# Leaving the k/v blocks of the second chunk out of the convolution's pacing account

## The chip, the cores and the metric

The kernel runs on one core of a Trainium2 chip. The metric is device microseconds of one execution, less is better. Engines are named as in the profile: PE (TensorE matmul), PEld (its weight loads), DVE (VectorE), ACT (ScalarE), POOL (GpSimd), SP (SyncE, whose queue issues the DMAs here).

## What is computed

One layer of a hybrid encoder over 16 meta tokens, a prompt of 256 tokens and a sample of 2048 tokens, all in float32. Cut to what matters:

```
h = rmsnorm(z)
q, k, v, g_att, c_val, c_glu, g_conv = split(h @ w_in)      # 1024 -> 2816 columns
att = windowed_gqa(rmsnorm(q), rmsnorm(k), v, sink) * silu(g_att)
u   = c_val * sigmoid(c_glu)
cnv = silu(layernorm(depthwise_conv31(u) + conv_b)) * silu(g_conv)
out = z + concat(att, cnv) @ w_out
```

The attention has 8 query heads and 2 key/value heads; a token sees the 16 meta tokens and the tokens at most 128 away. The convolution is 31 taps wide and runs per channel over 512 channels; its LayerNorm runs over the channels of a token.

## The kernel before

**Tiling.** The tokens stand in 18 blocks of 128 (b = 0 to 17), in six groups of three blocks, in two chunks of three groups. The input projection has eleven units of 256 columns; each matmul has float32r operands that are split in a high and a low part, three passes for each of eight slices of the 1024 inputs, so one output tile is 24 matmuls. For each chunk the program goes through the units in this order: four convolution units, two convolution gates, two attention gates, the k/v unit, two q units. `kv_group` calls `kv_block` for each block of 128 tokens: 24 matmuls into the PSUM tile pj, the norm of k (squares on ACT, `rsqrt` on POOL), the split and store of v, and in the next two ticks kn on DVE, a transpose kt on PE, ks on ACT and DVE, and the store to kd. In the second chunk it is called for blocks 9 to 17.

**Convolution.** For each chunk and each of four channel tiles, `conv` puts 31 taps in a queue; a tap is one DVE instruction over 128x1167 (line 946). They aren't written at once: `tick(ns)` is called after each piece of PE work with the time that the piece is taken to last, and pays taps from that credit; `owe(ns)` charges the credit with other DVE work, here 800 for a k/v block:

```
    def tick(ns):
        credit[0] += LOAD * ns
        if ln_q and not flushing[0] and ln_q[0][0]():
            ln_q.pop(0)[1]()
            ...
            credit[0] -= 800
        while credit[0] > 0 and (conv_q[0] or conv_q[1]):
            ...
            credit[0] -= cost
            f()
        credit[0] = min(credit[0], 0.0)
```

`tick` also writes what `later(k, f)` has put off by k ticks.

**LayerNorm of the convolution.** When the last taps of a chunk are written, `ready()` becomes true a set number of ticks later (one, for the second chunk), and each further tick writes one block of `ln_block`: four transposes lnt on PE (line 221), statistics on DVE, `rsqrt` on POOL, then in the next tick zn on DVE (line 234), then four transposes lnu back (line 240), SiLU on ACT into the same tile zn, and then the store of zn to the DRAM tile cd on SP (line 246). zn has three buffers, so the zn of a block waits for the store of the block three before it. There are ten such blocks in the second chunk.

**What stands around it.** After the fourth block of the last q unit but one, `attention_open` frees the convolution's space and loads the attention's constants, among them bias (1520 KB, line 269), then q, kw and v tiles. The first attention blocks are woven into the last q units: scores S (line 383), the exponential on ACT, a scaling on POOL (line 479), transposes pT_c, pT_m, pT_x (lines 495 and 499), their split in high and low by ACT and DVE (lines 515 and 516), the products O with v (line 533). When the projections are done, `attention_rest` goes on with attention and output projection y (line 609). For the boundary blocks pT_x is split and then spread by POOL (line 507); pm, which pT_x reads, has one buffer (line 470). cn on POOL (line 579) is the gate of the convolution half, mch and mcl its split (lines 586 and 587).

**What sets the order.** The instructions of an engine run in program order. That order is made by a scheduler at build time that moves instructions past each other after a time model of its own; POOL from `attention_open` on, and PE from `attention_rest` on, keep the order in which the program is written. All DMAs are issued by SP, in order, in eight lanes: an issue waits until the eighth before it has landed.

Of the kernel before, what the change touches and what calls it, by code (L numbers as in the profile page):

```python
# [85 lines left out]
CHUNKS = [[0, 1, 2], [3, 4, 5]]  # L86
# [13 lines left out]
def hymba_kernel(  # L100
# [58 lines left out]
    def owe(ns):  # L159
        credit[0] -= ns  # L160

    def later(k, f):
        due.setdefault(clock[0] + k, []).append(f)
# [30 lines left out]
    def store(dst, src):  # L194
        later(2, lambda: nc.sync.dma_start(dst, src))
# [505 lines left out]
    if True:  # L701
# [171 lines left out]
        def proj_te(ws, g, o, rows):  # L873
            x = xg[g]
            ps = pj()
            k = 0
            for d in range(ND):
                for wi, xi in PASSES:
                    nc.tensor.matmul(  # L879
                        ps[:rows, :UW],  # L880
                        x[xi][:, d, o : o + rows],
                        ws[:, d, wi, :],
                        start=(k == 0),
                        stop=(k == 3 * ND - 1),
                    )
                    k += 1
            return ps
# [87 lines left out]
        def head_norm(ps, rows, nh, tag, late=False):  # L975
            ss = gp.tile([P, 4], F32, tag="ss", name=f"ss{tag}", bufs=4)
            if phase[0] == 2 or tag.startswith("q0_9") or tag.startswith("q0_1"):
                sq = gp.tile([P, 4, HD], F32, tag="sq4", name=f"sq{tag}", bufs=2)
                sqf = sq.rearrange("p h e -> p (h e)")[:rows, : HD * nh]
                nc.scalar.activation(sqf, ps[:rows, : HD * nh], AF.Square)  # L980
                nc.vector.tensor_reduce(ss[:rows, :nh], sq[:rows, :nh, :], axis=AX.X, op=ALU.add)
            else:
                sq = gp.tile([P, 4, HD], F32, tag="sq4", name=f"sq{tag}", bufs=2)[:, 0, :]
                for h in range(nh):
                    nc.scalar.activation(  # L985
                        sq[:rows], ps[:rows, HD * h : HD * h + HD], AF.Square, accum_out=ss[:rows, h : h + 1]
                    )
            rq = gp.tile([P, 4], F32, tag="rq", name=f"rq{tag}", bufs=4)
            if late:
                later(late, lambda: rsqrt(rq[:rows, :nh], ss[:rows, :nh], 1.0 / HD, EPS))  # L990
            else:
                rsqrt(rq[:rows, :nh], ss[:rows, :nh], 1.0 / HD, EPS)
            return rq
# [29 lines left out]
        def kv_block(ws, g, o, rows, b):  # L1023
            ps = proj_te(ws, g, o, rows)
            rk = head_norm(ps, rows, KV, f"k{b}")
            vs = sp.tile([P, KV, 2, HD], F32R, tag="vs", name=f"vs{b}", bufs=3)
            pv = ps[:rows, P : 2 * P].rearrange("p (h e) -> p h e", e=HD)
            nc.scalar.copy(vs[:rows, :, 0, :], pv)
            nc.vector.tensor_tensor(vs[:rows, :, 1, :], pv, vs[:rows, :, 0, :], op=ALU.subtract)
            vflat = vs[:rows].rearrange("p a b e -> p (a b e)").bitcast(F32)  # L1030
            store(vmd if b < 0 else vd[b], vflat)
            kn = sp.tile([P, KV, HD], F32, tag="kn", name=f"kn{b}")
            owe(800)

            def fin():
                pk = ps[:rows, 0:P].rearrange("p (h e) -> p h e", e=HD)
                nc.vector.tensor_tensor(  # L1037
                    kn[:rows],
                    pk,
                    rk[:rows, :KV].unsqueeze(2).to_broadcast([rows, KV, HD]),  # L1040
                    op=ALU.mult,
                )
                later(1, fin2)

            def fin2():
                pt = psum.tile([P, 512], F32, tag="d", name=f"kt{b}")
                nc.tensor.transpose(pt[:, :rows], kn[:rows].rearrange("p a e -> p (a e)"), ident[:rows, :rows])
                ks = sp.tile([P, 2 * P], F32R, tag="ks", name=f"ks{b}")
                nc.scalar.mul(ks[:, :rows], pt[:, :rows], kscale[:, 0:1])
                nc.vector.scalar_tensor_tensor(  # L1050
                    ks[:, rows : 2 * rows], pt[:, :rows], kscale[:, 0:1], ks[:, :rows], op0=ALU.mult, op1=ALU.subtract
                )
                to = (kmd if b < 0 else kd[b]).rearrange("(h p) k l n -> p h k (l n)", h=2)
                for kv in range(KV):
                    part = ks[HD * kv : HD * kv + HD, : 2 * rows].bitcast(F32)
                    store(to[:, :, kv, :], part.unsqueeze(1).to_broadcast([HD, 2, 2 * rows]))

            later(1, fin)

        def kv_group(ws, g):  # L1060
            if g == 0:
                kv_block(ws, 0, 0, NM, -1)
                tick(24 * 107)
            for b in range(3 * g, 3 * g + 3):
                kv_block(ws, g, blk_local(b)[1], P, b)
                tick(24 * 110)
# [248 lines left out]
```

## Time and profile before

| what | value |
|---|---|
| median of 3 runs | 943.96 us (943.12 to 943.99) |
| profiled execution | 943.95 us, of which the span of the trace is 941.9 us |
| PE busy | 935.6 us, 99% of the span |
| DVE busy | 744.4 us, 79% |
| ACT busy | 421.8 us, 45% |
| POOL busy | 293.3 us, 31% |
| granted TensorE clock | 1.000 |

The span runs from the first to the last instruction; the 2.05 us between it and the execution's time lie around it. Busy time of PE is the time in which at least one matmul is in flight; matmuls overlap each other, so that a short hold of PE hardly shows in it and is read from the starts of matmuls that follow each other.

### The profile page before, as it was taken

To read this page: it belongs to the slowest core of one execution; us is meant where nothing else is said; L and a number is where in the kernel's file an instruction comes from. 1 tells how busy PE (TensorE), PEld (TensorE's weight loads), DVE (VectorE), ACT (ScalarE), POOL (GpSimd) and SP (SyncE) were. 2 spreads that over 40 slices of the span, in tenths; PEclk is the share of its full clock that TensorE was granted. 3 is DMA by queue.
4 is the path that set the end of the run, shared out by engine and by line. 5 is a ranking of instruction groups with operands and counts; after the bars stand their busy time and mean duration, and the time that the engine had idled before them with its cause. 6 is when DMAs were issued, how large, how long until landed. Compare 5 with 4: busy or idle time off the path is not lost.

```text
span 941.9 us, 16665 instructions
## 1 busy us (share of the span) xinstructions
PE 935.6 (99%) x5794; PEld 886.3 (94%) x5794; DVE 744.4 (79%) x1263; ACT 421.8 (45%) x1160; POOL 293.3 (31%) x490
## 2 busy tenths in 40 slices
PE   9999999999999999999999999999999999999998
PEld 8999999999999999999999999988888888888887
DVE  5579999997977879999996655677777677767773
ACT  7432022253457751011111356666666666656661
POOL 4320000173558400000000553755433242333332
PEclk9999999999999999999999999999999999999999
DMA  8575345676656595233333697975666556655512
GB/s 306 170 253 217 134 176 176 217 269 251 182 185 189 182 312 182 90 113 134 140 128 123 159 327 225 395 240 159 200 188 172 151 165 196 188 159 148 163 62 68
DMA packets 146211, 176.49 MB, mean 187 GB/s; under 512 B 40816, under 2 KB 108736, under 8 KB 146000
## 3 DMA queue, kind: packets, MB, share of 16 engines
q1 hardware_dynamic: 146128, 175.43, 57.8%
q8 instruction: 46, 0.75, 0.3%
q14 instruction: 37, 0.30, 0.1%
HBM read 112.69 MB, written 62.70 MB: 186 GB/s over the span
## 4 chain that ended last, share of the span: by engine, by line
PE 94%; DMA 2%; DVE 1%; SPq 1%; issue 0%; ACT 0%; POOL 0%; DVEq 0%; ACTq 0%; POOLq 0%
PE pj L863 43%; PE y L609 21%; PE pj L879 13%; PE O L533 5%; PE S L383 4%; PE pT_c L499 2%; PE pT_m L499 2%; PE pT_x L499 1%; DMA cd<-zn 1%; DMA bias<-in_bias_c 1%; PE qT L383 1%; PE lnu L240 0%; DMA xn<-in_z 0%; PE lnt L221 0%; DVE xt L772 0%
## 5 line engine op out<-in xcount | busy, mean ns | idle before, releaser
L863 PE MATMUL pj<-xh,ws 128*128 128x384 f32 (+1 forms) x1536 | 395.9, 338 | 0.1
L946 DVE SCALAR_TENSOR_TENSOR y<-us,cw,y 128x1167 f32<-128x1167 f32 x240 | 329.0, 1427 | 0.4
L863 PEld LDWEIGHTS pj<-xh,ws 128*128 128x128 f32 x1536 | 280.0, 188 | 0.4 <-ACT xh L1111 0.4
L863 PE MATMUL pj<-xl,ws 128*128 128x384 f32 (+1 forms) x768 | 260.9, 340 | 0.1
L609 PE MATMUL y<-wo,rest 128*128 128x512 f32 (+1 forms) x672 | 172.7, 394 | 0.0
L879 PE MATMUL pj<-ws,xh 128*128 128x256 f32 (+1 forms) x880 | 164.2, 284 | 0.3 <-DVE kn L1037 0.3
L863 PEld LDWEIGHTS pj<-xl,ws 128*128 128x128 f32 x768 | 144.1, 188 | 0.5 <-DVE xl L801 0.4
L609 PEld LDWEIGHTS y<-wo,rest 128*128 128x128 f32 x672 | 117.5, 189 | 21.4 <-DVE rest L566 0.3
L879 PEld LDWEIGHTS pj<-ws,xh 128*128 128x128 f32 (+1 forms) x880 | 136.1, 187 | 1.1 <-issue 0.4
L879 PE MATMUL pj<-ws,xl 128*128 128x256 f32 (+1 forms) x440 | 124.3, 283 | 0.0
L441 DVE CUSTOM_DVE_ANT_0 sb<-S,bias,vec 128x304 f32<-128x304 f32 (+5 forms) x144 | 74.5, 517 | 33.8 <-PE S L383 31.5
L453 ACT ACTIVATE sb<-sb,nm 128x304 f32<-128x304 f32 (+5 forms) x144 | 77.8, 540 | 48.9 <-DVE nm L441 48.2
L971 ACT ACTIVATE go<-pj 128x384 f32<-128x384 f32 x48 | 23.5, 489 | 149.8 <-PE pj L863 142.3
L879 PEld LDWEIGHTS pj<-ws,xl 128*128 128x128 f32 (+1 forms) x440 | 82.2, 187 | 0.2
L479 POOL TENSOR_SCALAR sb<-sb,es 128x304 f32<-128x304 f32 (+5 forms) x144 | 73.1, 525 | 16.0 <-DVE es L466 13.1
L561 POOL TENSOR_TENSOR at<-at,ga 128x256 f32<-128x256 f32 x36 | 26.5, 737 | 164.0 <-DVE at L555 104.8
L148 POOL TENSOR_SCALAR ssk<-ssk 128x2 f32<-128x2 f32 x18 | 8.4, 465 | 210.0 <-ACT sqk L985 210.0
L383 PEld LDWEIGHTS S<-kw,q 128*128 128x128 f32 x288 | 53.2, 188 | 10.6
L383 PE MATMUL S<-kw,q 128*128 128x304 f32 (+5 forms) x288 | 62.8, 299 | 0.0
L148 POOL TENSOR_SCALAR ssq<-ssq 128x4 f32<-128x4 f32 (+2 forms) x55 | 23.5, 427 | 98.3 <-ACT xn L726 74.4
L906 ACT ACTIVATE sg<-pj 128x384 f32<-128x384 f32 (+1 forms) x24 | 11.8, 492 | 82.9 <-PE pj L863 82.0
L609 PE MATMUL y<-wo,mch 128*128 128x512 f32 x144 | 47.2, 409 | 0.0
(139 smaller groups left out, 1306.9 us busy)
## 6 DMA issues: line engine op xcount, KB each, us to landing
wd<-ws SPq DMA_DIRECT2D x36, 512.0 KB, 5.8
ws<-wd SPq DMA_DIRECT2D x36, 512.0 KB, 6.2
wraw<-in_w_in SPq DMA_DIRECT2D x52, 256.0 KB, 6.3
xn<-in_z SPq DMA_DIRECT2D x18, 512.0 KB, 5.5
gd<-go SPq DMA_DIRECT2D x48, 192.0 KB, 2.2
yo<-in_z SPq DMA_DIRECT2D x36, 256.0 KB, 3.9
out_y<-yo SPq DMA_DIRECT2D x35, 256.0 KB, 2.7
wo<-wod SPq DMA_DIRECT2D x16, 512.0 KB, 7.4
```

Of the source, the lines that this page charges most:

```text
L148: nc.gpsimd.tensor_scalar(src, src, scale, eps, op0=ALU.mult, op1=ALU.add)
L383: r = f(*a, **k)
L441: nc.vector.tensor_tensor_reduce(out=sb[:, n, c0:c1], in0=ps[:, 0:w], in1=cst["bias"][:, kv, at + c0 : at + c1], scale=1.0, scalar=nsnk[:, ...
L453: nc.scalar.activation(sb[:, n, c0:c1], sb[:, n, c0:c1], AF.Exp, bias=nm[:, n : n + 1], scale=-1.0, accum_out=rs[:, n : n + 1],)
L479: nc.gpsimd.tensor_scalar(sb[:, k, a0:a1], sb[:, k, a0:a1], es[:, k : k + 1], 1.0, op0=ALU.mult, op1=ALU.mult)
L499: nc.tensor.transpose(pt[: c1 - c0, n, :], sbt[b, kv][:, n, c0:c1], ident)
L533: nc.tensor.matmul(opj[b, kv][:, n0:n1], t[:r, kv, :], p[:r, n0:n1], start=(k == "c" and i == 0), stop=(k == "x" and i == len(work) - 1),)
L561: nc.gpsimd.tensor_tensor(at[:, pr, :], at[:, pr, :], gat[b][:, pr, :], op=ALU.mult)
L609: nc.tensor.matmul(ps, mh[mi][:, e % 4, :], wo[e, wi][:, cols], start=(e == 4 and k == 0), stop=(e == 3 and k == 2),)
L863: nc.tensor.matmul(ps[:, :n], ws[:, d, wi, P * half_i : P * half_i + P], x[xi][:, d, o : o + n], start=(k == 0), stop=(k == 3 * ND - 1),)
L879: nc.tensor.matmul(ps[:rows, :UW], x[xi][:, d, o : o + rows], ws[:, d, wi, :], start=(k == 0), stop=(k == 3 * ND - 1),)
L946: nc.vector.scalar_tensor_tensor(y[:, yo + o0 : yo + o1], u[:, o0 + k : o1 + k], cw[:, j, k : k + 1], y[:, yo + o0 : yo + o1], op0=ALU.mul ...
```

## The change

`kv_block` charges its 800 to the credit only for the blocks of the first chunk.

```
             kn = sp.tile([P, KV, HD], F32, tag="kn", name=f"kn{b}")
-            owe(800)
+            owe(800 if g in CHUNKS[0] else 0)
```

The same instructions are issued, as many on each engine; their order differs on all five. Three places follow, each before and then after.

PE, at the end of the fifth k/v block of the second chunk (pj is the projection's tile, lnt the first LayerNorm transposes), before:

```order
L879 MATMUL pj_5333<-ws_8_4916,xl_3263 128x256
L879 MATMUL pj_5333<-ws_8_4916,xh_3262 128x256
L879 MATMUL pj_5378<-ws_8_4916,xh_3484 128x256
L879 MATMUL pj_5378<-ws_8_4916,xl_3485 128x256
L879 MATMUL pj_5378<-ws_8_4916,xh_3484 128x256 x2
```

and after:

```order
L879 MATMUL pj_5333<-ws_8_4916,xl_3263 128x256
L879 MATMUL pj_5333<-ws_8_4916,xh_3262 128x256
L221 MATMUL lnt_5369<-ident,y_0_3778 128x128
L221 MATMUL lnt_5369<-ident,y_1_3984 128x128
L221 MATMUL lnt_5369<-ident,y_2_4332 128x128
L221 MATMUL lnt_5369<-ident,y_3_4720 128x128
L879 MATMUL pj_5392<-ws_8_4916,xh_3484 128x256
```

The first LayerNorm block stands one k/v block, 24 matmuls, earlier. The order of the taps themselves on DVE, and the instructions that stand between the last of them, are the same before and after.

SP, around the load of bias (cd takes the finished LayerNorm blocks; the first of its stores here is the fifth of ten), before:

```order
L269 DMA bias<-in_bias_c 128x6080
L317 DMA vc_5856<-vd 128x256
L317 DMA vm_5857<-vd 128x256
L329 DMA q_6092<-qd 128x512
L195 DMA qd<-qs_11_5762 128x256
L300 DMA kw_5836<-kd 128x4x128 x2
L317 DMA vc_6570<-vd 128x256
L317 DMA vm_6571<-vd 128x256
L195 DMA qd<-qs_12_5821 128x256
L246 DMA cd<-zn_5703 128x512
```

and after:

```order
L269 DMA bias<-in_bias_c 128x6080
L317 DMA vc_5880<-vd 128x256
L317 DMA vm_5881<-vd 128x256
L246 DMA cd<-zn_5667 128x512
L195 DMA qd<-qs_11_5786 128x256
L329 DMA q_6093<-qd 128x512
L300 DMA kw_5860<-kd 128x4x128 x2
L246 DMA cd<-zn_5727 128x512
```

The fifth store to cd moves from the tenth to the third issue behind bias, the sixth from the fourteenth to the eighth.

PE, at the end of the input projection (S, pT and O belong to the first two attention blocks, y to the output projection), before; the 24 matmuls of the last projection tile, pj_6583, stand ahead of the first row, and the transposes pT_c_6621 and pT_m_6643 ahead of those:

```order
L879 MATMUL pj_6583<-ws_7_5574,xh_3484 128x256
L383 MATMUL S_1_1_6648<-kw_5836,q_1_6311 128x240 x2
L533 MATMUL O_1_6651<-ptiles,vc_5856 128x512
L533 MATMUL O_0_6467<-ptiles,vm 128x512
L533 MATMUL O_1_6651<-ptiles,vc_5856 128x512
L533 MATMUL O_1_6651<-ptiles,vm_5857 128x512
```

and after:

```order
L879 MATMUL pj_6583<-ws_7_5598,xh_3484 128x256
L499 MATMUL pT_c_6621<-ident,sb_5872 128x128 x4
L383 MATMUL S_1_0_6629<-kw_5860,q_1_6311 128x272 x2
L499 MATMUL pT_m_6643<-ident,sb_5872 128x128 x4
L383 MATMUL S_1_1_6648<-kw_5860,q_1_6311 128x240 x2
L533 MATMUL O_0_6467<-ptiles,vm 128x512
L533 MATMUL O_1_6651<-ptiles,vc_5880 128x512 x2
L533 MATMUL O_1_6651<-ptiles,vm_5881 128x512
```

The transposes have moved behind the last projection tile, right ahead of the products O_1 that read their split.

DVE at the same place, before:

```order
L441 ISA sb_5844,nm_1_6626<-S_1_0_6629,bias,vec 128x272
L441 ISA nm_1_6626 128x1
L465 TENSOR_TENSOR es_0_6414<-es_0_6414,rs_0_6413 128x4
L466 RECIPROCAL es_0_6414<-es_0_6414 128x4
L981 TENSOR_REDUCE ssq_16_6560<-sqq_16_6561 128x4
L516 TENSOR_TENSOR ptiles<-pT_c_6621,ptiles 128x512
L516 TENSOR_TENSOR ptiles<-pT_m_6643,ptiles 128x512
L587 TENSOR_TENSOR mcl<-cn_6257,mch 128x512
```

and after:

```order
L465 TENSOR_TENSOR es_0_6414<-es_0_6414,rs_0_6413 128x4
L466 RECIPROCAL es_0_6414<-es_0_6414 128x4
L981 TENSOR_REDUCE ssq_16_6560<-sqq_16_6561 128x4
L587 TENSOR_TENSOR mcl<-cn_6257,mch 128x512
L441 ISA sb_5868,nm_1_6626<-S_1_0_6629,bias,vec 128x272
L441 ISA nm_1_6626 128x1
L516 TENSOR_TENSOR ptiles<-pT_c_6621,ptiles 128x512
```

mcl and the scores' step of S_1_0 now stand ahead of the split of pT_c. On ACT, likewise, mch has moved from behind the two casts of line 515 to ahead of them; POOL's order at this place is the same.

## Rows read from the trace of the kernel before

**Rows 1.** The page: the span, and busy time of each engine.
```profile
span 941.9 us, 16665 instructions
...
PE 935.6 (99%) x5794; PEld 886.3 (94%) x5794; DVE 744.4 (79%) x1263; ACT 421.8 (45%) x1160; POOL 293.3 (31%) x490
```

**Rows 2.** Stretch: length, busy of PE, PEld, DVE, ACT, POOL; clock; DMA share, GB/s.
```profile
560.00:580.00 20.00, 19.30 (x164) 18.91 (x164) 9.24 (x20) 11.28 (x32) 8.23 (x20) 1.00 0.73 231
```

**Rows 3.** Timeline of PE (start, length): ahead of the eighth and tenth lnu.
```profile
567.31 0.28 PE L879 MATMUL pj<-ws,xh 128*128 128x256 f32 x1
567.64 0.66 PE L240 MATMUL lnu<-ident,zn 128*128 128x128 f32 x4
...
574.29 0.28 PE L879 MATMUL pj<-ws,xh 128*128 128x256 f32 x1
575.22 0.63 PE L240 MATMUL lnu<-ident,zn 128*128 128x128 f32 x4 [0.66 <-DVE zn L234]
```

**Rows 4.** Timeline of DVE: the eighth and tenth zn, and what they waited for.
```profile
566.77 0.81 DVE L234 TENSOR_SCALAR zn<-lnt,mv 128x512 f32<-128x512 f32 x1 [3.07 <-DMA cd<-zn]
...
574.27 0.81 DVE L234 TENSOR_SCALAR zn<-lnt,mv 128x512 f32<-128x512 f32 x1 [4.00 <-DMA cd<-zn]
```

**Rows 5.** Timeline of SP: issues behind bias; the last is the fifth store to cd.
```profile
552.29 0.70 SPq L269 DMA_DIRECT2D bias<-in_bias_c  x1
...
553.99 0.43 SPq L329 DMA_DIRECT2D q<-qd  x1
...
561.77 0.33 SPq L317 DMA_DIRECT2D vm<-vd  x1
...
562.93 0.36 SPq L246 DMA_DIRECT2D cd<-zn  x1
```

**Rows 6.** DMA views around 552.3 and 554.0: KB, us from issue to landing.
```profile
bias<-in_bias_c SPq DMA_DIRECT2D x1, 1520.0 KB, 9.5
...
q<-qd SPq DMA_DIRECT2D x1, 256.0 KB, 9.1
```

**Rows 7.** Chain that ended last, pieces (start, length): PE's pace.
```profile
531.36 0.44 PE lnt L221 x4
...
602.26 2.84 PE pj L879 x24
```

**Rows 8.** Timeline of PE: the ninth lnt.
```profile
562.15 0.60 PE L221 MATMUL lnt<-ident,y 128*128 128x128 f32 x4
```

**Rows 9.** Timeline of DVE: the last tap of the convolution.
```profile
522.75 1.42 DVE L946 SCALAR_TENSOR_TENSOR y<-us,cw,y 128x1167 f32<-128x1167 f32 x1
```

**Rows 10.** Timeline of POOL: from the release of pm to line 507.
```profile
597.56 0.40 POOL L470 TENSOR_TENSOR pm<-sb,es 128x128 f32<-128x128 f32 x1 [1.77 <-issue]
...
601.21 1.28 POOL L579 TENSOR_TENSOR cn<-cn,gc 128x512 f32<-128x512 f32 x1
602.45 1.22 POOL L507 TENSOR_TENSOR ptiles<-ptiles,vec 128x512 fp32r<-128x512 f32 x1
```

**Rows 11.** Timeline of ACT: the cast mch.
```profile
604.86 0.63 ACT L586 CAST mch<-cn 128x512 fp32r<-128x512 f32 x1
```

**Rows 12.** Timeline of DVE: the scores' step of S_1_0, split of pT_c, mcl.
```profile
602.70 0.49 DVE L441 CUSTOM_DVE_ANT_0 sb<-S,bias,vec 128x272 f32<-128x272 f32 x1
...
604.13 0.68 DVE L516 TENSOR_TENSOR ptiles<-pT_c,ptiles 128x512 fp32r<-128x512 f32 x1
...
605.53 0.69 DVE L587 TENSOR_TENSOR mcl<-cn,mch 128x512 fp32r<-128x512 f32 x1
```

**Rows 13.** Timeline of PE: pT_x of the first block, then around the last projection tile.
```profile
597.15 0.27 PE L495 MATMUL pT_x<-ident,pm 128*128 128x128 f32 x1
...
604.94 0.39 PE L383 MATMUL S<-kw,q 128*128 128x240 f32 x2
605.16 0.40 PE L533 MATMUL O<-ptiles,vc 128*128 128x512 f32 x1
605.39 0.39 PE L533 MATMUL O<-ptiles,vm 128*128 128x512 f32 x1
605.62 0.40 PE L533 MATMUL O<-ptiles,vc 128*128 128x512 f32 x1
```

## The prediction

> **What bounds the kernel now.** I read the page first: PE is busy 99% of the span and DVE 79% [rows 1]. So the end is set by the stream of matmuls, and the change, which adds and takes away no instruction, can only move the time by the holds of PE between matmuls. Next I looked for those in the stretch that the change reorders, from about 510 us to 610 us, by stages: one stage of 20 us, from 560 us, is the only one in which PE isn't busy throughout, 19.30 of 20.00 [rows 2]. The timeline of PE there shows two holds, both ahead of a LayerNorm transposition lnu. A matmul of the projection starts 2.84 / 24 = 0.118 us after the one before it [rows 7]; ahead of the eighth lnu 567.64 - 567.31 = 0.33 us pass, 0.21 too many, and ahead of the tenth 575.22 - 574.29 = 0.93, 0.81 too many [rows 3]. Together 1.02 us: all that this stretch can give back. Who held them: zn on DVE, which itself waited for a store to cd, 3.07 us and 4.00 us, to free its buffer [rows 4]. And that store was late because SP stood still: the eighth issue behind bias is issued at 561.77, when bias lands (552.29 + 9.5 = 561.8), and the fifth store to cd comes two issues after that, at 562.93 [rows 5, 6].
>
> **The change, part by part.** *The taps.* The diff means to let the last taps follow each other on DVE. The order says that the scheduler had already put them as it puts them now: the last tap ran at 522.75 for 1.42 us [rows 9], with the same neighbours before and after. Worth nothing. What does change is that `ready` comes a tick sooner, so all ten LayerNorm blocks stand one k/v block earlier against PE's stream. The first lnt moves from 531.36 to 531.36 - 24 x 0.118 = 528.5; the last tap ends at 524.2, so 4.3 us of cover are left [rows 7, 9]; were that cover gone, PE would wait for the tap itself.
>
> *The eighth lnu.* In the order before, 41 matmuls stand between the ninth lnt and the eighth lnu, now 11, with as many transpositions ahead as before. PE arrives at 562.15 + 0.44 + 11 x 0.118 = 563.9 [rows 7, 8], some 3.5 us sooner than it did. Its zn must be done by then, and for that the fifth store must have landed. On SP this store is now the third issue behind bias. The third issue before was q, of the same 256 KB, and it landed at 553.99 + 9.1 = 563.1 [rows 5, 6]. I take that for the store. Then zn runs from 563.2 to 564.0 (0.81 us, [rows 4]), lnu goes at 564.06 (before, 567.64 - 567.58 = 0.06 after zn, [rows 3, 4]), and PE waits about 0.2 us. Bounds: 0, if bias lands half a microsecond sooner; 1.0, if it lands 0.8 us later, since the weights ahead of it are asked for when PE ends the k/v unit, and two more groups of transpositions (0.44 us each, [rows 7]) now stand ahead of that point.
>
> *Does the queue keep its order?* The landings of bias and q follow their issue [rows 5, 6]. The Trainium skill, in "DMA: Bandwidth & Descriptors", section "Queues, rings and completion order", says that completion is not in order for one issuing engine; by that rule the store could land ahead of bias, and the sum would lose its 0.2 us.
>
> *The ninth and tenth lnu.* Bias to q is 512 KB (two transfers of 128 KB and q) in 1.3 us, 394 KB per us [rows 5, 6]. The sixth store is the eighth issue behind bias, so issued at 561.8; behind the fifth store lie 896 KB and its own 256 KB, 2.9 us: it lands at 566.0, its zn ends near 566.9. PE arrives 23 matmuls and two groups later, 564.06 + 2.7 + 0.88 = 567.6 [rows 7]. The seventh store stands 768 KB further: 566.0 + 2.6 = 568.6, its zn ends at 569.5, PE arrives at 567.6 + 0.44 + 31 x 0.118 = 571.7. No wait at either, 0.7 and 2.2 us to spare, by estimate. So of the 1.02 us about 0.8 come back.
>
> *The end of the projection.* Here the change costs. Before, the transpositions pT_c and pT_m of the second attention block's half stood ahead of the last projection tile, whose 24 matmuls, 2.84 us [rows 7], hid their split on ACT and DVE. Now they stand behind it, and between pT_c and the products O_1 lie only two S, pT_m and one O. Measured from pT_x of the first half (597.15, [rows 13]): PE needs 0.11 for it, 0.23 for an O, 41 x 0.118 = 4.85 for the projection, 0.22 for an S (605.16 - 604.94), and pT_c starts at 5.4; then 0.44, 0.22, 0.44, 0.22 bring O_0 at 6.7, and two O of 0.23 (605.62 - 605.39) bring the second O_1, which reads the low part, at 7.2 [rows 7, 13]. POOL is released by the same pT_x and runs through: line 579 ends 602.49 - 597.15 = 5.3 after it, line 507 at 603.67, 6.5 after it [rows 10, 13]. O_0 needs line 507: 0.2 to spare. The low part needs, on ACT and DVE in the new order, mch (0.63, to 5.95), mcl (0.69, to 6.65), the scores' step of S_1_0 (0.49, to 7.15) and the split of pT_c (0.68, to 7.8) [rows 11, 12]. So PE waits about 0.6 us. Before, that split ended at 604.81 and its O came at 605.62 [rows 12, 13]. Bounds: 0, if DVE's four steps overlap or POOL starts sooner; 1.3, if POOL's chain comes 0.7 later, for then O_0 waits too. It can't be below nothing, as nothing here held PE before. Behind this place the attention's order is the same again, save one O and a few loads; I count nothing for it.
>
> *Sum*, against the profiled execution of 943.95 us, which is the median of the runs to 0.01: 943.95 - 1.02 + 0.2 + 0.6 = 943.7.
>
> **The rivals.**
> *Both waits gone.* The fifth store lands in time and the split of pT_c isn't late: 943.95 - 1.02 = 942.9. For it: both of my waits are a few tenths on a chain of five or six rows. Against it: DVE's four steps in a row are in the order, and POOL's release hangs on pT_x.
> *Nothing happens to the time.* What the LayerNorm gives, the end of the projection takes to the tenth, or the early blocks are held by bias as much as before: 943.95. It can't be told from the forecast by the time, only by the rows.
> *Slower: the eighth lnu is early and its store is not.* If the fifth store lands as late as before, just ahead of 566.77 [rows 4], PE, which now comes 3.5 us sooner, stands from 563.9 to 567.64: 3.7 us, and the time is 943.95 - 1.02 + 3.7 + 0.6 = 947.2. This counts as slower (above 945.84) once lnu waits over 2.3 us, that is, once the store lands after 565.3. For it: the store waits for SiLU of the fifth block, and all of SP's queue waits behind it. Against it: it needs 2.2 us more than the row of q gives.
> *More waits at both ends*, short of that: 1.0 and 1.3 in place of 0.2 and 0.6 give 945.2.
>
> **How the numbers follow.** The forecast, with waits within some tenths of mine, 0.69; both gone 0.12; waits near their upper bounds 0.08; the slower rival 0.08; something that I don't see and that gains over 0.2%, 0.03, as no hold of that size is in the stretch. The range reaches from the case with both waits gone to just short of their upper bounds, 942.9 to 945.0. A measurement of this kernel can tell about 0.2%, 1.89 us, from no change: faster 0.03, within 0.2% 0.89, slower 0.08.
>
> **What would show it.** In the changed profile: the taps as before; the first lnt near 528.5; no hold of PE ahead of the tenth lnu, and a few tenths at the eighth; the fifth store issued within a few us of bias and landing about 1.3 us behind it; pT_c right behind the last projection matmul, and the second O_1 some 0.6 us late, with the split of pT_c on DVE ending just ahead of it. I am wrong if PE holds over 1 us ahead of any lnu, if the O_1 products run without a gap, or if a wait turns up in the k/v blocks, where LayerNorm's statistics now stand among one more block's kn and v.

## The result, and the profile after

The changed kernel took 945.7 us (median of 16 runs, 943.98 to 947.47), the kernel before 943.96 (16 runs beside them, 943.09 to 944.86): a ratio of 1.0019, interval 1.0012 to 1.0027. It is slower, by about 1.7 us, where 943.7 was forecast with a range up to 945.0. Two later comparisons of the same two kernels gave 1.0014 (1.0002 to 1.0026) and 1.0017 (1.0007 to 1.0027), with medians 0.55 and 1.56 us apart. (Every ratio is the one on record, with its 95% interval; it is not the quotient of the two medians.)

The page of the profiled execution, which took 946.34 us (span, busy time):

```profile
span 944.4 us, 16656 instructions
...
PE 937.2 (99%) x5794; PEld 888.2 (94%) x5794; DVE 744.9 (79%) x1263; ACT 422.1 (45%) x1160; POOL 295.5 (31%) x490
```

Busy shares say as little as before [rows 1]. Two things move the span. The first projection matmul starts at 13.15 us here and at 12.20 in the profile before: 0.95 us of the 2.5 between the spans lie in the head of the program, which the change doesn't touch (in the later profiles it starts between 12.17 and 13.26 whichever kernel it is). Counted from there, the span is 931.3 us after and 929.7 before: 1.6 us, close to the difference of the medians. These lie in two holds, that is, delays of PE read from the starts of matmuls that follow each other. The view of what PE waited for (us in total, times, longest) names them; it counts idle time alone, which is less:

```profile
PE lnu L240 <- DVE zn L234: 1.3, 1, 1.3
PE O L533 <- DVE ptiles L516: 0.8, 1, 0.8
```

**The eighth lnu.** In the timeline of PE, the counterpart of [rows 3], the matmul of the projection that stands ahead of it starts at 564.69, and lnu 1.62 us later where 0.12 would do: a hold of 1.50 us, in place of 0.21. The tenth has none (574.10 - 573.97 = 0.13 us), in place of 0.81.

```profile
564.69 0.28 PE L879 MATMUL pj<-ws,xh 128*128 128x256 f32 x1
566.31 0.65 PE L240 MATMUL lnu<-ident,zn 128*128 128x128 f32 x4 [1.35 <-DVE zn L234]
...
573.97 0.28 PE L879 MATMUL pj<-ws,xl 128*128 128x256 f32 x1
574.10 0.60 PE L240 MATMUL lnu<-ident,zn 128*128 128x128 f32 x4
```

The chain that ended last names the cause in three pieces (start, length): the fifth store to cd is under way for 9.59 us, and zn and lnu follow it.

```profile
555.73 9.59 DMA cd<-zn
...
565.44 0.82 DVE zn L234
...
566.31 0.65 PE lnu L240 x4
```

SP issues it 1.66 us behind bias, where before 10.6 us passed [rows 5]; the wait has moved from SP's lanes into the queue, where the store stands behind bias:

```profile
554.07 0.62 SPq L269 DMA_DIRECT2D bias<-in_bias_c  x1
...
555.73 0.38 SPq L246 DMA_DIRECT2D cd<-zn  x1
```

**The second O_1.** PE again, around the end of the projection, the counterpart of [rows 13]: from the first O_1 to the second 1.23 us pass, where 0.23 would do.

```profile
599.81 0.27 PE L495 MATMUL pT_x<-ident,pm 128*128 128x128 f32 x1
...
605.20 0.60 PE L499 MATMUL pT_c<-ident,sb 128*128 128x128 f32 x4
...
606.84 0.40 PE L533 MATMUL O<-ptiles,vc 128*128 128x512 f32 x1
608.07 0.50 PE L533 MATMUL O<-ptiles,vc 128*128 128x512 f32 x1 [0.84 <-DVE ptiles L516]
```

What it waits for, on POOL, then ACT, then DVE (the counterparts of [rows 10], [rows 11] and [rows 12]): cn ends at 605.44, mch follows it at 605.48, mcl follows mch at 606.13, the scores' step and the split of pT_c follow mcl, and the split ends at 608.02:

```profile
603.88 1.56 POOL L579 TENSOR_TENSOR cn<-cn,gc 128x512 f32<-128x512 f32 x1
605.41 1.04 POOL L507 TENSOR_TENSOR ptiles<-ptiles,vec 128x512 fp32r<-128x512 f32 x1
```

```profile
605.48 0.62 ACT L586 CAST mch<-cn 128x512 fp32r<-128x512 f32 x1 [1.22 <-POOL cn L579]
606.01 0.58 ACT L515 CAST ptiles<-pT_c 128x512 fp32r<-128x512 f32 x1
```

```profile
603.88 0.43 DVE L1010 TENSOR_TENSOR qr<-qr,rqq 128x256 f32<-128x256 f32 x1 [0.92 <-POOL rqq L149]
604.22 1.25 DVE L465 TENSOR_TENSOR es<-es,rs 128x4 f32<-128x4 f32 x1
...
606.13 0.86 DVE L587 TENSOR_TENSOR mcl<-cn,mch 128x512 fp32r<-128x512 f32 x1 [0.15 <-ACT mch L586]
606.92 0.49 DVE L441 CUSTOM_DVE_ANT_0 sb<-S,bias,vec 128x272 f32<-128x272 f32 x1
...
607.34 0.68 DVE L516 TENSOR_TENSOR ptiles<-pT_c,ptiles 128x512 fp32r<-128x512 f32 x1
```

The account: -1.02 for the two old holds, +1.50 and +1.00 for the new ones, 1.48 of the 1.6 us.

### The profile page after: what moved, and what is told of

Read it like the earlier page. It is cut to its first block, busy times and chain, and to the rows that moved or that the text cites. A ratio compares the mean times of both kernels' runs of the same rounds, so it can differ in the third digit from the quotient of the medians.

```text
span 944.4 us, 16656 instructions
## 1 busy us (share of the span) xinstructions
PE 937.2 (99%) x5794; PEld 888.2 (94%) x5794; DVE 744.9 (79%) x1263; ACT 422.1 (45%) x1160; POOL 295.5 (31%) x490
## 4 chain that ended last, share of the span: by engine, by line
PE 92%; DMA 3%; DVE 1%; SPq 1%; POOL 1%; issue 1%; ACT 0%; DVEq 0%; POOLq 0%; ACTq 0%
PE pj L863 43%; PE y L609 21%; PE pj L879 12%; PE O L533 5%; PE S L383 4%; DMA cd<-zn 2%; PE pT_c L499 2%; PE pT_m L499 2%; PE pT_x L499 1%; PE qT L383 1%; DMA wraw<-in_w_in 1%; PE lnu L240 1%; PE lnt L221 1%; DMA qd<-qr 1%; DVE xt L772 0%
## 5 line engine op out<-in xcount | busy, mean ns | idle before, releaser
L148 POOL TENSOR_SCALAR ssq<-ssq 128x4 f32<-128x4 f32 (+2 forms) x55 | 25.4, 462 | 95.8 <-ACT xn L726 71.7
```

Source lines behind the costliest of these rows:

```text
L148: nc.gpsimd.tensor_scalar(src, src, scale, eps, op0=ALU.mult, op1=ALU.add)
```

## The experiments

The theory: the loss is these two holds, the first set by when bias lets the fifth store through, the second by what stands ahead of the split of pT_c. The rival: something spread (transfers in contention, the head). The changed kernel needs no separate test of its parts: the kernel before with LayerNorm set one tick earlier (0 in place of 1) gives the same order on all five engines, row for row but for the numbers in names, and the changed kernel with LayerNorm one tick later gives that of the kernel before. So the charge of 800 acts through that one tick alone.

All times below are medians beside runs of the kernel before on the same chip. Against the rival speaks one sum over all thirteen profiles of this document: counted from the first projection matmul, their spans lie between 929.2 and 931.3 us; less the holds that are named here, between 928.6 and 929.1.

**Four zn buffers in the changed kernel.**

```diff
-            st["zn"] = yp.tile([P, 512], F32, tag="zn", name=f"zn{b}", bufs=3)
+            st["zn"] = yp.tile([P, 512], F32, tag="zn", name=f"zn{b}", bufs=4)
```

> The changed kernel with four zn buffers in place of three: the eighth zn then waits for the fourth store to cd, which is issued ahead of bias, and no longer for the fifth. Theory (the 1.74 us are two holds of PE, 1.51 us ahead of the eighth lnu and 1.00 us at the second O_1, less the 1.02 us of the old holds): no hold of PE over 0.1 us ahead of any lnu. In the order, mch and mcl still stand ahead of the split of pT_c, but 48 projection matmuls stand between pT_x and pT_c in place of 41, 0.83 us more, so about 0.5 us of the 1.00 stay at the second O_1. Time about 945.7 - 1.5 - 0.5 = 943.7. Rival (the time lies in something spread, as contention of the transfers or the head of the program): about 945.7, with the holds gone or not.

944.06 us against 944.36, ratio 1.0000 (0.9992 to 1.0009). No lnu holds PE, and 0.56 us stay at the second O_1. As the theory has it: with the first hold gone and the second nearly halved, no loss is measured. The hold at O_1, in the timeline of PE:

```profile
605.32 0.40 PE L533 MATMUL O<-ptiles,vc 128*128 128x512 f32 x1
606.11 0.50 PE L533 MATMUL O<-ptiles,vc 128*128 128x512 f32 x1 [0.40 <-DVE ptiles L516]
```

**bias in two halves.**

```diff
-        nc.sync.dma_start(bias, bias_c)
+        nc.sync.dma_start(bias[:, 0], bias_c[:, 0]); later(4, lambda: nc.sync.dma_start(bias[:, 1], bias_c[:, 1]))
```

> The changed kernel with three zn buffers, and bias loaded in two halves of 760 KB: the first where all of it was, the second behind the fifth store to cd. Theory (the store lands late since the bytes of bias stand ahead of it in the queue): the fifth store lands 760 / 394 = 1.9 us sooner against PE's stream, its zn is done before PE comes, and the hold of 1.51 us at the eighth lnu goes; at the second O_1 about 0.5 us stay, as 48 matmuls stand there in place of 41. Time about 943.7. Rival (the store is late because of its own issue, behind the SiLU of its block or the lanes, and not because of bias): it lands as late as in the changed kernel, the hold stays at 1.5 and the time is about 945.2.

945.87 us against 944.36, ratio 1.0018 (1.0009 to 1.0027), where 943.7 was forecast: the hold stays, at 1.6 us, and 0.57 at the second O_1. But not for the rival's reason. The first half lands after 7.6 us and the store 1.4 us behind it, at 562.86 in place of 565.20 (against the same start of the projection), 2.3 us sooner. What I had overlooked in the order is that with two loads the scheduler puts the eighth lnu 21 matmuls, 2.5 us, earlier as well. PE arrives at 562.2 and waits as long as before. The timeline of DVE, then of PE:

```profile
562.98 0.81 DVE L234 TENSOR_SCALAR zn<-lnt,mv 128x512 f32<-128x512 f32 x1 [4.63 <-DMA cd<-zn]
```

```profile
562.02 0.38 PE L221 MATMUL lnt<-ident,y 128*128 128x128 f32 x2
...
563.85 0.66 PE L240 MATMUL lnu<-ident,zn 128*128 128x128 f32 x4 [1.45 <-DVE zn L234]
```

So the hold does not follow the landing alone, but the landing less PE's coming. What the missing bytes are worth, forecast at 1.9 us, isn't shown by this one profile: beside the five of the table below, in which bias is whole, the store lands 0.4 to 2.3 us sooner.

**The convolution half gated a slot later in the changed kernel,** twice.

```diff
-        if has_b and slot == (MSLOT if s_ > 1 else 2):
+        if has_b and slot == (MSLOT if s_ > 1 else 3):
```

> The changed kernel with the convolution half of the first output block gated one slot later, so that on POOL line 507 stands ahead of line 579, on ACT the cast of pT_c ahead of mch, and on DVE the split of pT_c ahead of mcl. The rest of the order is that of the changed kernel. Theory (mch and mcl ahead of the split hold the second O_1): the hold of 1.00 us at O_1 goes, 0.2 to 0.4 us may come up at the first product y, which needs mcl, and the 1.51 us at the eighth lnu stay. Time about 945.7 - 1.0 + 0.2 = 944.9. Rival (O_1 waits for something else, as the S step or POOL): the hold stays near 1.0 and the time is 945.7.

> a_ms3 once more, unaltered, for a second profile. Theory (its missing hold at the eighth lnu was the luck of one execution, in which bias took 8.3 us to land): bias takes 9 to 10 us here and lnu holds PE by 0.5 to 1.5 us, if bias is slow again; the hold at the second O_1 is 0.2 us as before. Rival (the edit itself takes the hold away): none at lnu and bias at 8.3 us again.

943.98 us against 944.36, ratio 1.0002 (0.9993 to 1.0011), where 944.9 was forecast with the first hold in place, and the second time 944.35 against 943.81, 1.0011 (1.0001 to 1.0021). The hold at the second O_1 is 0.23 us in both profiles, in place of 1.00: with mch and mcl behind the split of pT_c, only the scores' step of S_1_0 is left ahead of it. y is not held. The surprise was the first profile: no hold at the eighth lnu, though nothing in the order ahead of it had changed.

```profile
564.05 0.28 PE L879 MATMUL pj<-ws,xh 128*128 128x256 f32 x1
564.17 0.60 PE L240 MATMUL lnu<-ident,zn 128*128 128x128 f32 x4
```

In the second it is back, at 0.47 us, just under the 0.5 to 1.5 forecast. The edit had not taken it away.

**Both kernels again, unaltered.**

> The changed kernel once more, unaltered, beside the next three. In a_ms3, whose order up to 560 us is that of the changed kernel, bias took 8.3 us to land in place of 9.7 and the hold at the eighth lnu was gone. Theory (that hold hangs on how fast the transfers of one execution run, and lies between 0 and about 2 us from one execution to the next): the times spread over 2 to 3 us, more than those of the kernel before (943.1 to 946.2) or of a_zn4 (943.4 to 944.7), the median is 1 to 1.7 us above the kernel before, and the hold at the second O_1 is 1.0 us in any execution. Rival (a_ms3 lost the hold by its edit): the hold is 1.5 us again and the spread is that of the kernel before.

> The changed kernel for a third profile. Theory (the eighth lnu goes 0.99 us after the landing of the fifth store, and PE comes 39.4 us after the first LayerNorm-stage matmul whatever the execution): hold between 0 and 1.6 us, equal to the landing of the store less PE's coming plus 0.99; hold at the second O_1 again 1.00. Rival (both holds are fixed by the order): 1.5 and 1.0.

> The kernel before once more, unaltered, for a second profile. Theory: its holds at the eighth and tenth lnu hang on the same transfers; they lie between 0 and 1.5 us together, 1.02 in the first profile. Rival (they are fixed): 0.2 and 0.8 us again, to 0.1. Time about 944.4, as in the runs beside the last four kernels.

The changed kernel gave 944.99 us against 944.44 and 945.37 against 943.81; its runs lie between 943.95 and 950.69, and between 944.23 and 946.55. The first of these medians is 0.55 us above, where 1 to 1.7 was forecast; and but for the one run at 950.69 its times spread hardly wider (2.8 us) than those of the kernel before (2.7), where a wider spread was forecast. The kernel before against itself gave 943.91 against 944.44, ratio 0.9995 (0.9985 to 1.0005): half a microsecond between two such medians need be no difference. The hold at the second O_1 is 1.00 us in all three of its profiles; that at the eighth lnu is 1.50, 1.04 and 0.44. The third profile:

```profile
563.82 0.28 PE L879 MATMUL pj<-ws,xh 128*128 128x256 f32 x1
564.38 0.66 PE L240 MATMUL lnu<-ident,zn 128*128 128x128 f32 x4 [0.28 <-DVE zn L234]
```

Five profiles now have the same order up to that lnu. The table counts us from the first projection matmul of each, which takes the head out; the hold is the start of lnu less the start of the last matmul, less 0.12:

| profile | bias, issue to landing | fifth store lands | last matmul ahead of lnu | lnu | hold |
|---|---|---|---|---|---|
| changed, first | 9.7 | 552.17 | 551.54 | 553.16 | 1.50 |
| changed, second | 9.8 | 551.73 | 551.56 | 552.72 | 1.04 |
| changed, third | 8.9 | 551.10 | 551.53 | 552.09 | 0.44 |
| gate later, first | 8.3 | 550.19 | 551.67 | 551.79 | 0 |
| gate later, second | 9.3 | 551.13 | 551.53 | 552.12 | 0.47 |

PE comes at the same time to 0.14 us. The store lands within a band of 2.0 us, and where it lands late enough lnu follows 0.99 us behind it (0.12 to the start of zn, 0.87 from there). This settles the first hold: its size is set by the landing. Where the band comes from is open, but hardly from what is ahead of bias: on the same clock the last transfer ahead of it lands between 543.97 and 544.71 in the five profiles, and bias between 4.57 and 6.26 us behind that. (The 39.4 us in the expectation of the third profile is a slip of mine; from the first lnt, 529.20, to the last matmul, 564.69, it is 35.5.)

The second profile of the kernel before shows its two old holds again, 0.26 and 0.78, so that my theory that these swing from 0 to 1.5 us has nothing for it: in both profiles their store is issued only after bias has landed, and they came out alike to 0.05 us. But it has a third one, of 0.8 us, at the last projection tile: PE, then ACT,

```profile
602.95 0.38 PE L879 MATMUL pj<-ws,xh 128*128 128x256 f32 x1 [0.57 <-ACT sqq L980]
```

```profile
602.24 0.37 ACT L1004 COPY qr<-pj 128x256 f32<-128x256 f32 x1 [3.00 <-DMA qd<-qr]
```

where ACT's copy waited 3.00 us for a store to qd, against 1.66 in the first profile, in which PE was not held. So the kernel before isn't fixed at 1.02 us of holds either; how often this third one comes isn't known.

**Four zn buffers in the kernel before,** the same edit as in the first experiment.

> The kernel before with four zn buffers, the 800 charged in both chunks. LayerNorm stands where it stood before, but the order at the end of the projection is that of the changed kernel: pT_c and pT_m behind the last projection tile, mch and mcl ahead of the split. Theory: both old holds at lnu go (1.02 us), and a hold of about 0.5 us turns up at the second O_1, although the pacing account is untouched: 943.96 - 1.02 + 0.5 = 943.4. Rival (the O_1 hold comes with the earlier LayerNorm and not with that order): no hold at O_1, 942.9.

944.65 us against 944.36, ratio 1.0007 (0.9998 to 1.0015). Its old holds at lnu are gone and 0.86 us turn up at the second O_1, although LayerNorm stands where it did: the O_1 hold comes with the place of pT_c behind the last projection tile, which this edit brings too, and not with the earlier LayerNorm. The forecast of 943.4 was too low: 0.86 in place of 0.5, and no gain is measured, where 0.17 us was left by the holds.

**Four buffers and the gate two slots earlier,** in both kernels.

```diff
-            st["zn"] = yp.tile([P, 512], F32, tag="zn", name=f"zn{b}", bufs=3)
+            st["zn"] = yp.tile([P, 512], F32, tag="zn", name=f"zn{b}", bufs=4)
...
-        if has_b and slot == (MSLOT if s_ > 1 else 2):
+        if has_b and slot == (MSLOT if s_ > 1 else 0):
```

> The changed kernel with four zn buffers and the convolution half of the first output block gated two slots earlier: line 579 then stands ahead of line 470 on POOL, and mch and mcl lie ahead of the transposition of pT_c by some 5 us. Theory (two holds are all that the change costs): no hold of PE over 0.2 us from 510 us on; time about 1.0 us below the kernel before, which keeps its holds at lnu: 943.3 where that has 944.4. Rival (the gate earlier makes POOL late for pm, or cn has not landed): a hold of 0.5 us or more at O_0, O_1 or y, and 944 or more.

> The kernel before with the same two edits, four zn buffers and the gate two slots earlier, the 800 charged in both chunks. Theory (where LayerNorm stands against PE's stream is worth nothing once zn has room): the same time as a_zn4ms0 to 0.3 us, about 943.3, and no hold over 0.2 us from 510 us on. Rival (the earlier LayerNorm gives or costs something of its own): the two differ by more than 0.5 us.

943.53 us with the change, 944.09 without it, against 944.44, where 943.3 was forecast for both: ratios 0.9993 (0.9984 to 1.0001) and 1.0000 (0.9991 to 1.0008). No hold at lnu; but 0.57 us stay at O_1 in both, with mch and mcl out of the way. So the second half of my theory was too narrow. ACT and DVE of the changed one:

```profile
602.99 0.37 ACT L1004 COPY qr<-pj 128x256 f32<-128x256 f32 x1 [1.70 <-PE pj L879]
603.25 0.39 ACT L980 ACTIVATE sqq<-pj 128x256 f32<-128x256 f32 x1
603.53 0.59 ACT L515 CAST ptiles<-pT_c 128x512 fp32r<-128x512 f32 x1
```

```profile
604.10 0.41 DVE L981 TENSOR_REDUCE ssq<-sqq 128x4 f32<-128x256 f32 x1
604.43 0.68 DVE L516 TENSOR_TENSOR ptiles<-pT_c,ptiles 128x512 fp32r<-128x512 f32 x1
```

Now the copy, the square and the sum of the last projection tile stand ahead: the cast on ACT ends at 604.12, and the split waits longer, for the scores' step and the sum on DVE (from 603.67 to 604.51). The same sum stood there with four buffers alone, where mcl ended at 604.64, just as the step began (604.62): the 0.56 us there met the forecast of 0.5, but not by mch and mcl. From the end of pT_c to the second O_1 PE has some 1.4 us of its own work (607.07 - 605.64 in the changed kernel), and the cast and the split alone take 0.59 and 0.68. What else is put ahead of the split shows as a hold: 0.23 with the scores' step, 0.57 with that and the tile's sum, 1.00 with mch, mcl and the step. That the two kernels differ by 0.6 us with equal holds isn't explained (0.3 was the most that was forecast); their intervals overlap.

**Five buffers, LayerNorm a tick later than before.**

```diff
-LN_WAIT = (9, 1)
+LN_WAIT = (9, 2)
...
-            st["zn"] = yp.tile([P, 512], F32, tag="zn", name=f"zn{b}", bufs=3)
+            st["zn"] = yp.tile([P, 512], F32, tag="zn", name=f"zn{b}", bufs=5)
```

> The kernel before with five zn buffers and LayerNorm a tick later, not earlier. The transpositions pT_c and pT_m then stand ahead of the last projection tile, as in the kernel before, and each zn waits for the store five blocks before it. Theory (zn's room and the place of pT_c are what counts): no hold at any lnu, none at O_1, so 1.0 us below the kernel before: 943.4 where that has 944.4; below a_zn4ms0, which kept 0.57 us at O_1, by some tenths. Rival (a later LayerNorm makes the last stores to cd and the load of cn late): a hold of 1 us or more in the attention, and 945 or more.

944.34 us against 943.81, ratio 1.0005 (0.9995 to 1.0014): no hold at lnu, none at O_1, and yet no gain, where 1.0 us was forecast. PE is held by about 1.0 us (0.80 of it idle) at the last projection tile, on the store to qd that held the kernel before in its second profile (ACT's copy waits 3.42 us for it). The forecast had no term for this wait. No version was measured faster than the kernel before beyond its interval; the nearest is the changed kernel with both edits, at 0.9993.

## Why the prediction was wrong, point by point

The measured 945.7 us lies 0.7 above the range. The places, the order and the waits were the ones forecast; two terms of the sum were too small, the 0.2 us at the eighth lnu (1.50 in the first profile) and the 0.6 at the end of the projection (1.00).

**The taps: right.** The first lnt starts at 529.20; less the 0.95 us of the head that is 528.25, against 528.5 forecast. Nothing holds PE there.

**The eighth lnu: the mechanism right, the term mis-sized.** PE was to come at 563.9 and came at 564.69 + 0.12 - 0.95 = 563.86. (The 11 matmuls that the prediction puts between the ninth lnt and lnu are counted from the ninth lnt's old place; in the new order half of that lnt stands later, and 21 lie between.) The fifth store was to land at 563.1, 1.3 us behind a bias that lands at 561.8. That step failed: I took the landing of bias, and of a store behind it, from the rows of one execution as fixed. On the clock of the profile before (the column of landings in the table plus 12.20) the store landed at 564.4, 563.9 and 563.3 in the changed kernel. The hold was 1.50, 1.04 and 0.44, against 0.2 with a bound of 1.0. The text let bias come 0.8 us later for the sake of the weights ahead of it; but the transfers ahead of it were no later than before (the last landed at 543.97 to 544.71 on the clock of the table, in the kernel before at 544.74). A hold can't be negative, so a landing that swings by 2 us also costs a little more than its middle value says: over the five profiles of the table the mean hold is 0.69 us, where the mean landing would give 0.57. Neither was in the sum.

**The queue's order: right.** In all thirteen profiles the transfers issued between 540 and 572 us, some 40 in each, landed in the order of their issue, and so did all the others of each profile. The rule cited from the Trainium skill ("DMA: Bandwidth & Descriptors", "Queues, rings and completion order") allows another order; none was seen here.

**The ninth and tenth lnu: right.** No hold at either in any profile of the changed kernel.

**The end of the projection: right in every link, 0.6 for 1.00.** POOL's line 579 started 4.07 us after pT_x, as before (4.06), but took 1.56 in place of 1.28, and mcl took 0.86 in place of 0.69: 0.45 us, about the error (the split ended 608.02 - 599.81 = 8.21 after pT_x, against 7.8). Line 579 began at the same moment as a multiplication on DVE, line 1010, and mcl while line 507 ran on POOL (below). mch, mcl, the step and the split then followed each other as listed.

**The range and the chances.** By the bound of 0.2% the result still counts as within it (1.0019), for which the chance was 0.89; but the intervals of all three comparisons lie above 1, so the sign of the forecast was wrong. The range let only one of the two terms come near its bound, or both with 8 in 100 (945.2). Both came high together in the first profile, and the median lies as high. The slower rival as priced (the store landing as late as before, 3.7 us) didn't happen: what happened is a landing between the forecast's and that one.

**What stays open:** counted from the first projection matmul, the three profiles of the changed kernel are 1.6, 1.2 and 0.6 us above the first profile before, and their holds explain 1.48, 1.02 and 0.42. Up to 0.2 us lie in gaps too small to name. The three medians are 1.7, 0.55 and 1.56 us above; with the mean first hold of the three profiles, 0.99, the sum would be 943.95 - 1.02 + 0.99 + 1.00 = 944.9. Whether the rest lies in longer holds of the executions that weren't profiled or elsewhere isn't shown. The gains that the holds leave to the five kernels with more buffers, 0.1 to 0.5 us, are too small for these comparisons to show.

## What to carry to other kernels

Where an engine's wait ends at the landing of a transfer that stands behind a large load, treat the landing as a spread and not as a row: take several executions, and cost the wait as the mean of the single waits, none of them under nothing. When a change shifts one chain against another, list every step between the new place of the producer and its consumer: here 1.4 us of cover were left for a chain of 1.3, so most of each further step ahead of it was paid (0.34 us for a sum of 0.41). And print the order of an experiment before it is costed: giving a buffer or splitting a load moved other work too.

## What the runs showed of the hardware

The time from issue to landing of one and the same load, 1520 KB, was 8.3 to 9.8 us in five executions with an identical order up to there.

A DVE instruction with two SBUF operands and a POOL one held each other up, though not everywhere. The 128x4 addition of line 465 on DVE took 0.15 us where POOL was idle (the changed kernel with four buffers and the gate two slots earlier), but in the changed kernel 1.25 us beside line 579 on POOL, and ended 0.03 us after it (605.47 and 605.44; the rows stand in the section on the result); in the kernel before it took 0.58 us and ended 0.03 us after line 507 (603.70 and 603.67). It goes the other way too: line 579 took 1.56 us where line 1010 on DVE began at the same moment and took 0.43; in the changed kernel with four buffers line 579 began 0.04 us ahead (601.35 and 601.39) and took 1.29, and line 1010 took 1.53. That is what the Trainium skill says in "SBUF — State Buffer", section "SBUF: two separate sides": the pair of ports that the two share goes wholly to whichever starts first. These rows agree. Others don't, or only in part: mcl began at 606.13, while line 507 ran on POOL until 606.45, and grew by 0.17 us, not by the 0.32 that were left; and in the kernel before the same addition at 591.65 took 0.15 us beside line 149 on POOL, which ran from 591.54 to 592.56.
